# A two-layer decoder trunk: constants loaded between weights, a new pace of splits, scaling and rotation as queued steps

## The chip, the core and the metric

The kernel runs on one core of one Trainium2 chip. TensorE (PE) multiplies, VectorE (DVE), ScalarE (ACT) and GpSimd (POOL) do the rest, and SyncE (SP) issues every DMA, in order, on one queue. Every engine works through its own instructions in the order in which the program lists them; semaphores make one wait for another. The metric is the device time of one launch in microseconds.

## The reference, cut to what matters

```python
x <- LayerNorm(alpha * x + concat(A, B) @ w_out0)      # layer 0
x <- LayerNorm(alpha * x + concat(C, D) @ w_out1)      # layer 1
# A: gated linear attention over chunks, with a low-rank decay gate; B: spatial gating in chunks of 128
# C: retention over chunks of 128, q and k turned by rotary positions; D: causal pooling, windows 2, 4, 8, 16
# each branch times silu of a gate; all of them from one product h = x @ w_in of their layer
def _layer_norm(x, g, b):
    mu = mean(x); var = mean((x - mu) ** 2)
    return (x - mu) * rsqrt(var + 1e-5) * g + b
def _rotary(x, positions):
    return concatenate([x1 * cos - x2 * sin, x1 * sin + x2 * cos])
```

x is 2048 tokens of 1024 float32. The input product of layer 0 has 3088 columns, that of layer 1 has 3072, each output product 1024.

## The kernel before, in words

The 2048 tokens are worked through in four blocks of 512 (`NB`), each block through both layers before the next. A block has four token tiles of 128.

**Products.** All large products go through `unit` (L162). One call is a product with 512 columns (272 or 256 for layer 0's v), summed over eight k-tiles, for four output tiles. Each float32 operand is held as two parts in fp32r, a high one and the rest, and three products of parts (`PASSES`) make one. `width` says how many output tiles are built side by side, each in a PSUM bank of the pool "big" (four banks). After the matmuls of a group, `evac` is called for each of its output tiles, and then `between`.

**Weights.** All tiles of weights come in one list, `stream`, in the order of use: for each block eight tiles of 272 columns of wv, four pairs of 256 columns, then fourteen weights of eight tiles. `fetch` (L102) issues the load of the next one into a buffer of a pool of seven, shared with the loads of x. `cut` (L112) splits a landed tile: ScalarE writes the high part (L89), VectorE the rest (L90); then it fetches the next. There is room for twelve split tiles (`SLOTS`); `room` counts what is free. `pace` (L122), called after each k-tile of a product, adds a credit for the matmuls done and cuts one tile for each whole credit, as long as there is room. So splits stand in the queues of ScalarE and VectorE between the other work, at places that the program fixes.

**Steps.** `later(fn, delay)` puts a piece of work on a list. `between` (L145) counts every entry down by one, collects those that are due, in the order in which they were queued, and runs them. It is called after each group of output tiles, and inside a product of `width` over 1 also after every KT/width k-tiles. A step that is queued while steps run is not counted down in that call.

**The start.** Eight tiles of x and eight of wv are loaded in turn and split (L278). Then come the loads of pv and w_a2 (three copies), five fetches (the four pairs, of two DMAs each, and the first tile of the next weight), and seven more constants (L288 to L299). In block 0 the first product (wv, 272 columns) has width 4, so it fills all four banks; its `evac_v0` (L451) copies 16 columns of each bank three times on VectorE and 256 columns on ScalarE (L457). The second product (256 columns) follows.

**LayerNorm.** `layer_norm_out` (L207) runs the output product as two units of 512 columns. The first has width 2, the second width 1. `evac` of the second half of a token tile adds the residual (L217), takes the statistics (L218, L221), has GpSimd make 1/sqrt (L196, L199), and scales the row in two VectorE operations (L226 with mean and gain, L228 with 1/sqrt and bias). `after` follows: in layer 0 it queues `turn` (L620), which transposes the row on TensorE into two PSUM banks of a pool of two and splits them (L626 on ScalarE, L627 on VectorE), so that they are the input of layer 1; in layer 1 it stores the row.

**Rotation.** The first product of layer 1 (q and k, width 1) is evacuated by `evac_qk` (L639): a copy on ScalarE (L644), and six operations on VectorE (L645 to L654); then a transposing `turn` (L656) is queued with delay 3. The turns of token tiles 2 and 3 of the LayerNorm fall between the units of this product.

Of the kernel before, what the change touches and what calls it, by code (L numbers as in the profile page):

```python
# [13 lines left out]
ALU = mybir.AluOpType  # L14
# [3 lines left out]
P = 128  # L18
SEQ = 2048
D = 1024  # L20
KT = D // P
TB = 512
# [7 lines left out]
SLOTS = 12  # L30
# [21 lines left out]
def trunk(ctx, tc, x, xT, pos, wv, w, w_a2, pvec, rowp, sgu_rows, w_sT, w_pool, ropec, poolc, out):  # L52
    nc = tc.nc
# [20 lines left out]
    def big():  # L74
        return ps_big.tile([P, 512], F32, tag="big", name="big")
# [4 lines left out]
    def w2(name):  # L80
        return work.tile([P, TB], F32, tag="w2", name=name)
# [13 lines left out]
    for b in range(NB):  # L95
        stream += [(wv[kt, :, 0:272],) for kt in range(KT)]
        stream += [(wv[kt, :, 272:528], wv[kt + 1, :, 272:528]) for kt in range(0, KT, 2)]
        stream += [(w[g, kt],) for g in ORDER for kt in range(KT)]
    landed, ready = [], []
    room, credit = [SLOTS], [0.0]  # L100

    def fetch():  # L102
        if not stream:
            return
        src = stream.pop(0)
        raw = rawp.tile([P, 512], F32, tag="raw", name="raw")
        width = src[0].shape[1]
        for i, s in enumerate(src):
            nc.sync.dma_start(raw[:, i * width:(i + 1) * width], s)
        landed.append((raw, len(src), width))  # L110

    def cut():  # L112
        raw, n, width = landed.pop(0)
        assert room[0] > 0
        room[0] -= 1
        t = wpool.tile([P, 2, 512], F32R, tag="w", name="wt")
        c = n * width
        split(raw[:, 0:c], t[:, 0, 0:c], t[:, 1, 0:c])
        ready.extend((t[:, :, i * width:(i + 1) * width], i == n - 1) for i in range(n))
        fetch()  # L120

    def pace(matmuls):  # L122
        credit[0] = min(credit[0] + matmuls / 6.0, 2.0)
        while credit[0] >= 1.0 and room[0] > 0 and landed:
            cut()
            credit[0] -= 1.0

# [14 lines left out]
    def later(fn, delay=1):  # L142
        steps.append([delay, fn])
# [18 lines left out]
    def unit(xs, evac, token_major, width=2, cols=512):  # L162


        wt = []
        for n in range(0, 4, width):
            ps = [big()[:, 0:cols] for _ in range(width)]
            for kt in range(KT):
                if len(wt) == kt:
                    while not ready:  # L170
                        cut()
                    wt.append(ready.pop(0))
                t, last = wt[kt]
                for i, p_ in enumerate(ps):
                    sl = slice((n + i) * P, (n + i + 1) * P)
                    xt = xs[kt // 4][:, kt % 4]
                    for q, (a, b) in enumerate(PASSES):
                        lhsT, rhs = (xt[:, a, sl], t[:, b, :]) if token_major else (t[:, a, sl], xt[:, b, :])
                        nc.tensor.matmul(p_, lhsT=lhsT, rhs=rhs, start=(kt == 0 and q == 0),  # L179
                                         stop=(kt == KT - 1 and q == 2))  # L180
                if n + width == 4 and last:
                    room[0] += 1
                pace(3 * width * cols / 512.0)
                if width > 1 and (kt + 1) % (KT // width) == 0 and kt < KT - 1:
                    between()
            for i, p_ in enumerate(ps):
                evac(n + i, p_)
            between()
# [18 lines left out]
    def layer_norm_out(xs, rows, lnrow, after, cuts=1):  # L207
        ln = r8.tile([P, 2, D], F32, tag="r8", name="ln")
        for i in range(2):
            nc.sync.dma_start(ln[:, i, :], rowp[lnrow + i:lnrow + i + 1, :].broadcast_to([P, D]))  # L210
        gt, bt = ln[:, 0, :], ln[:, 1, :]
        sts = [small.tile([P, 2, 6], F32, tag="lnst", name="lnst", bufs=5) for _ in range(NT)]

        def evac(half, t, ps):
            row = rows[t // 2][:, t % 2, :]
            rh = row[:, half * 512:half * 512 + 512]
            nc.vector.scalar_tensor_tensor(rh, rh, ALPHA, ps, op0=ALU.mult, op1=ALU.add)  # L217
            nc.vector.bn_stats(sts[t][:, half, :], rh)  # L218
            if half == 1:
                mv = small.tile([P, 2], F32, tag="lnmv", name="lnmv")  # L220
                nc.vector.bn_aggr(mv, sts[t])  # L221
                rs = small.tile([P, 1], F32, tag="lnrs", name="lnrs")
                rstd(rs, mv[:, 1:2], LN_EPS)
                for c in range(0, D, D // cuts):
                    cs = slice(c, c + D // cuts)
                    nc.vector.scalar_tensor_tensor(row[:, cs], row[:, cs], mv[:, 0:1], gt[:, cs],  # L226
                                                   op0=ALU.subtract, op1=ALU.mult)
                    nc.vector.scalar_tensor_tensor(row[:, cs], row[:, cs], rs, bt[:, cs], op0=ALU.mult, op1=ALU.add)  # L228
                    after(t, row, cs)

        unit(xs, lambda t, ps: evac(0, t, ps), True)
        unit(xs, lambda t, ps: evac(1, t, ps), True, width=1)
# [24 lines left out]
    pv = const.tile([P, 20], F32, name="pv")  # L257
    gla_g, sgu_g, ret_g, pool_s, b_a = (pv[:, 4 * i:4 * i + 4] for i in range(5))
    wa2 = const.tile([48, 256], F32R, name="wa2")
    wsT = const.tile([P, 4, P], F32, name="wsT")  # L260
    wp = const.tile([P, 2, TB], F32R, name="wp")
    rope = const.tile([P, 32 + 10], F32, name="rope")
    poolt = const.tile([P, 4, 16], F32, name="poolt")
# [6 lines left out]
    pi_t = const.tile([P, 16], I32, name="pi_t")  # L270
    pf = const.tile([P, 16], F32, name="pf")

    wa2raw = w2("wa2raw")[0:48, 0:256]
    wraw, sb, sbs = w2("wraw"), w2("sgub"), w2("sgubs")
# [3 lines left out]
    for kt in range(KT):  # L278
# [3 lines left out]
        raw, _, width = landed.pop(0)  # L282
        t = wpool.tile([P, 2, 512], F32R, tag="w", name="wt")
# [1 line left out]
        room[0] -= 1  # L285
        ready.append((t[:, :, 0:width], True))

    nc.sync.dma_start(pv, pvec)  # L288
    for i in range(3):
        nc.sync.dma_start(wa2raw[16 * i:16 * i + 16, :], w_a2)  # L290
    for _ in range(5):
        fetch()
    nc.sync.dma_start(wsT, w_sT)
    nc.sync.dma_start(wraw, w_pool.rearrange("p g c -> p (g c)"))
    nc.sync.dma_start(sb, sgu_rows[0:1, :].broadcast_to([P, TB]))
    nc.sync.dma_start(sbs, sgu_rows[1:2, :].broadcast_to([P, TB]))
    nc.sync.dma_start(rope, ropec)
    nc.sync.dma_start(poolt, poolc)
    nc.sync.dma_start(pi_t, pos)  # L299

    def constants():

# [141 lines left out]
    def layer0(b, xs):  # L444
# [30 lines left out]
                nc.vector.tensor_copy(f[:, s, 3:4], e2[:, 3, 1:2])  # L475

        unit(xs, evac_v0, True, width=4 if b == 0 else 2, cols=272)
        if b == 0:
            constants()
            later(constants2, 3)  # L480
            later(constants3, 4)
# [137 lines left out]
        def after(t, row, cs):  # L619
            def turn():  # L620
                for c in range(2):
                    pt = tr()
                    for k in range(4):
                        nc.tensor.transpose(pt[:, k, :], row[:, (4 * c + k) * P:(4 * c + k + 1) * P], ident)  # L624
                    hi = x1[c][:, :, 0, t * P:(t + 1) * P]
                    nc.scalar.activation(hi, pt, AF.Copy)  # L626
                    nc.vector.tensor_tensor(x1[c][:, :, 1, t * P:(t + 1) * P], pt, hi.bitcast(F32), op=ALU.subtract)  # L627
            later(turn, 3)

        layer_norm_out([ca, cb], rows, 0, after)  # L630
        return x1, rows
# [1 line left out]
    def layer1(b, xs, rows):  # L633
# [3 lines left out]
        kst = [ks[t // 2][:, t % 2, :] for t in range(NT)]  # L637

        def evac_qk(t, ps):  # L639
            g = b * NT + t  # L640
            a = w2("ra")
            s_ = w2("rs_")

            nc.scalar.activation(a[:, 0:256], ps[:, 0:256], AF.Copy)  # L644
            nc.vector.tensor_tensor(a[:, 256:512].rearrange("p (h c) -> p h c", c=64),  # L645
                                    ps[:, 256:512].rearrange("p (h c) -> p h c", c=64),
                                    gam[:, 4:8].unsqueeze(2).broadcast_to([P, 4, 64]), op=ALU.mult)
            a3 = a.rearrange("p (h c) -> p h c", c=32)
            s3 = s_.rearrange("p (h c) -> p h c", c=32)
            nc.vector.tensor_tensor(s3, a3, sin[:, g:g + 1, :].broadcast_to([P, 16, 32]), op=ALU.mult)  # L650
            nc.vector.tensor_tensor(a3, a3, cos[:, g:g + 1, :].broadcast_to([P, 16, 32]), op=ALU.mult)
            nc.vector.tensor_tensor(a3[:, 0::2, :], a3[:, 0::2, :], s3[:, 1::2, :], op=ALU.subtract)
            nc.vector.tensor_tensor(a3[:, 1::2, :], a3[:, 1::2, :], s3[:, 0::2, :], op=ALU.add)
            nc.vector.tensor_copy(kst[t], a[:, 256:512])  # L654

            def turn():  # L656
                pt = tr()
                for s in range(4):
                    nc.tensor.transpose(pt[:, s, :], a[:, s * P:(s + 1) * P], ident)  # L659
                nc.scalar.activation(qkT[:, t], pt, AF.Copy)  # L660

            later(turn, 3)

        unit(xs, evac_qk, True, width=1)

# [91 lines left out]
        def after(t, row, cs):  # L757
            nc.sync.dma_start(out[b * TB + t * P:b * TB + (t + 1) * P, cs], row[:, cs])
# [90 lines left out]
```

## Time and profile before

| what | value |
|---|---|
| median of 3 runs | 1519.88 us (1518.55 to 1520.22) |
| the profiled execution | 1519.84 us, its span 1518.1 us, mean granted clock 0.993 |
| VectorE, ScalarE, GpSimd busy | 932.2, 554.9, 132.1 us |
| DMA | 162.18 MB, mean 107 GB/s |

The page of the profile gives each engine's busy time; the view of waits says who waited for whom, in total, how often and at most; the timeline lists instructions as start, duration, engine, line, operation, and in brackets the idle time before them with what ended it; the view of windows gives each engine's busy time in a stretch, then the granted clock, the DMA engines' busy share and GB/s. PEld is TensorE's weight load, SPq is the issuing of a DMA by SP.

### The profile page before, as it was taken

The numbers are of one execution on the slowest core, as the hardware profiler recorded it, in microseconds if no ns is written. First come the engines' busy times: TensorE is split into PE (matmuls) and PEld (weight loads), VectorE is DVE, ScalarE is ACT, GpSimd is POOL, SyncE is SP. The second block draws the span as 40 slices with busy tenths as digits, with TensorE's granted clock in tenths as the row PEclk, the third lists the DMA queues.
The fourth block names the chain that finished last, engine by engine and source line by source line (L and its number), as shares of the span: only waits on it lengthen the run. The fifth ranks groups of instructions, "written<-read, shape, count | busy, mean of one in ns | idle before, by whom it ended". The sixth has DMA issues, their size and how long they took to land.

```text
span 1518.1 us, 20883 instructions
## 1 busy us (share of the span) xinstructions
PE 1486.5 (98%) x7728; PEld 1247.3 (82%) x7728; DVE 932.2 (61%) x1860; ACT 554.9 (37%) x956; POOL 132.1 (9%) x184
## 2 busy tenths in 40 slices
PE   6999999999999999999999999999999999999997
PEld 6888878888988887888898888788889888878886
DVE  4486475657656558565675646847576554684756
ACT  5534323334443332324254332333426334142430
POOL 1020010100101001010001100101010110100001
PEclk8999999999999999999999999999999999999999
DMA  7323422224522442322453233131435315222321
GB/s 235 96 72 116 135 78 91 67 84 155 181 83 86 136 133 63 96 72 81 144 181 97 84 126 125 56 111 57 135 112 171 112 56 170 81 91 76 93 82 55
DMA packets 87046, 162.18 MB, mean 107 GB/s; under 512 B 10096, under 2 KB 18336, under 8 KB 86944
## 3 DMA queue, kind: packets, MB, share of 16 engines
q1 hardware_dynamic: 86944, 160.85, 33.3%
q8 instruction: 60, 0.98, 0.3%
q14 instruction: 42, 0.34, 0.1%
HBM read 152.43 MB, written 8.39 MB: 106 GB/s over the span
## 4 chain that ended last, share of the span: by engine, by line
PE 92%; DVE 3%; DMA 1%; POOL 1%; issue 1%; ACT 1%; SPq 0%; POOLq 0%; DVEq 0%; ACTq 0%
PE big L179 82%; PE att L356 4%; PE trp L392 1%; DVE wt L90 1%; PE trp L572 1%; PE trp L624 1%; PE trp L711 1%; POOL lnrs L196 1%; DMA raw<-in_w 1%; DVE T L627 1%; ACT wt L89 0%; DVE lnst L218 0%; PE trp L659 0%; PE trp L747 0%; PE trp L599 0%
## 5 line engine op out<-in xcount | busy, mean ns | idle before, releaser
L179 PE MATMUL big<-wt,T 128*128 128x512 f32 (+2 forms) x3456 | 728.1, 370 | 14.1 <-ACT v L457 9.5
L179 PEld LDWEIGHTS big<-wt,T 128*128 128x128 f32 x3456 | 601.0, 190 | 121.5 <-ACT v L457 9.7
L179 PE MATMUL big<-T,wt 128*128 128x512 f32 x2688 | 625.8, 391 | 0.0
L179 PEld LDWEIGHTS big<-T,wt 128*128 128x128 f32 x2688 | 500.6, 188 | 106.3 <-issue 2.7
L90 DVE TENSOR_TENSOR wt<-raw,wt 128x512 fp32r<-128x512 f32 (+1 forms) x496 | 320.8, 673 | 236.7 <-ACT wt L89 234.8
L89 ACT ACTIVATE wt<-raw 128x512 fp32r<-128x512 f32 (+1 forms) x496 | 298.3, 616 | 366.3 <-PE big L179 252.2
L196 POOL TENSOR_SCALAR lnrs<-lnmv 128x1 f32<-128x1 f32 x32 | 39.9, 1248 | 618.9 <-DVE lnmv L221 618.9
L217 DVE SCALAR_TENSOR_TENSOR rows<-rows,big 128x512 f32<-128x512 f32 x64 | 43.6, 681 | 53.6 <-PE big L179 53.6
L199 POOL TENSOR_TENSOR rs<-rs,neghalf 128x4 f32<-128x4 f32 x48 | 58.4, 1216 | 3.9
L228 DVE SCALAR_TENSOR_TENSOR rows<-rows,lnrs,ln 128x1024 f32<-128x1024 f32 (+1 forms) x36 | 42.0, 1166 | 24.9 <-POOL lnrs L199 24.8
L626 ACT ACTIVATE T<-trp 128x512 fp32r<-128x512 f32 x32 | 17.8, 596 | 82.3 <-PE trp L624 82.1
L218 DVE BATCH_NORM_STATS2 lnst<-rows 128x6 f32<-128x512 f32 x64 | 44.5, 695 | 2.2
L371 DVE COPY_PREDICATED pm<-mask,att 128x256 f32<-128x256 int32 x64 | 24.6, 439 | 30.8 <-PE att L356 30.8
L226 DVE SCALAR_TENSOR_TENSOR rows<-rows,lnmv,ln 128x1024 f32<-128x1024 f32 (+1 forms) x36 | 42.0, 1166 | 1.1
L204 DVE SCALAR_TENSOR_TENSOR y<-trp,pv,sg 128x512 f32<-128x512 f32 x48 | 33.7, 744 | 12.4 <-PE trp L599 7.0
L719 ACT ACTIVATE pb<-big 128x512 f32<-128x512 f32 x16 | 9.4, 590 | 76.4 <-PE big L179 76.4
L584 ACT ACTIVATE act<-big 128x512 f32<-128x512 f32 x32 | 18.3, 597 | 51.7 <-PE big L179 50.9
L682 DVE BATCH_NORM_STATS2 st<-att 128x6 f32<-128x128 f32 x64 | 14.2, 285 | 35.4 <-PE att L356 35.4
L356 PEld LDWEIGHTS att<-v,pm 128*128 128x128 f32 x256 | 33.5, 191 | 2.4
L550 DVE BATCH_NORM_STATS2 st<-zt 128x6 f32<-128x128 f32 x64 | 13.7, 277 | 35.1 <-ACT zt L546 35.1
L89 ACT ACTIVATE T<-y 128x512 fp32r<-128x512 f32 x48 | 29.4, 627 | 15.7 <-DVE y L204 15.3
L724 DVE TENSOR_TENSOR pl<-pb 128x527 f32<-128x527 f32 x16 | 11.3, 708 | 38.6 <-ACT pb L719 37.8
(184 smaller groups left out, 905.8 us busy)
## 6 DMA issues: line engine op xcount, KB each, us to landing
raw<-in_w SPq DMA_DIRECT2D x448, 256.0 KB, 2.8
xraw<-in_xT SPq DMA_DIRECT2D x32, 256.0 KB, 3.5
rows<-in_x SPq DMA_DIRECT2D x8, 1024.0 KB, 7.1
ln<-in_rowp SPq DMA_DIRECT2D x16, 512.0 KB, 6.4
out<-rows SPq DMA_DIRECT2D x12, 512.0 KB, 2.7
raw<-in_wv SPq DMA_DIRECT2D x32, 136.0 KB, 3.2
raw<-in_wv SPq DMA_DIRECT2D x32, 128.0 KB, 2.8
out<-rows SPq DMA_DIRECT2D x8, 256.0 KB, 2.0
```

Source lines behind the costliest of these rows:

```text
L89: nc.scalar.activation(hi, src, AF.Copy)
L90: nc.vector.tensor_tensor(lo, src, hi.bitcast(F32), op=ALU.subtract)
L179: nc.tensor.matmul(p_, lhsT=lhsT, rhs=rhs, start=(kt == 0 and q == 0), stop=(kt == KT - 1 and q == 2))
L196: nc.gpsimd.tensor_scalar(dst, var, eps, None, op0=ALU.add)
L199: nc.gpsimd.tensor_tensor(dst, dst, neghalf[:, :n], op=ALU.pow)
L204: nc.vector.scalar_tensor_tensor(y, psT, gain, sil, op0=ALU.mult, op1=ALU.mult)
L217: nc.vector.scalar_tensor_tensor(rh, rh, ALPHA, ps, op0=ALU.mult, op1=ALU.add)
L218: nc.vector.bn_stats(sts[t][:, half, :], rh)
L226: nc.vector.scalar_tensor_tensor(row[:, cs], row[:, cs], mv[:, 0:1], gt[:, cs], op0=ALU.subtract, op1=ALU.mult)
L228: nc.vector.scalar_tensor_tensor(row[:, cs], row[:, cs], rs, bt[:, cs], op0=ALU.mult, op1=ALU.add)
L356: nc.tensor.matmul(dst, lhsT=lhsT, rhs=rhs, start=start, stop=stop, skip_group_check=True)
L371: nc.vector.copy_predicated(pm[t % 2][:, r::2, :], mask_b, ps[r][:, 2:4, :])
```

## The change

Four things are altered:
- Constants. A list `small_loads` is filled after the loads of x and wv, and each later `fetch` issues one of its loads behind its own. Its order is w_a2 (three), pv, wraw, wsT, sb, sbs, rope, poolt, pos.
- Pace. `cut` is held back while `room` is not over `hold`, which is set to SLOTS - KT - KT//2 at the start and to 0 after the first product of each block. In a product of width 4 the credit of a k-tile is 0.75 instead of 3·width·cols/512/6.
- LayerNorm. The two scaling operations and `after` become a step, `scale`, queued with delay 1. The first of them takes the whole row; the second is still cut in `cuts` pieces.
- Rotation. All of `evac_qk` becomes a step, `rotate`, queued with delay 1. Both kinds of `turn`, now queued from inside a step, get delay 2 instead of 3.

```diff
-    landed, ready = [], []
-    room, credit = [SLOTS], [0.0]
+    landed, ready, small_loads = [], [], []
+    room, credit, hold = [SLOTS], [0.0], [0]
...
         landed.append((raw, len(src), width))
+        if small_loads:
+            nc.sync.dma_start(*small_loads.pop(0))
...
-        while credit[0] >= 1.0 and room[0] > 0 and landed:
+        while credit[0] >= 1.0 and room[0] > hold[0] and landed:
...
-                pace(3 * width * cols / 512.0)
+                pace(3 * width * cols / 512.0 if width < 4 else 0.75 * 6)
...
-                for c in range(0, D, D // cuts):
-                    cs = slice(c, c + D // cuts)
-                    nc.vector.scalar_tensor_tensor(row[:, cs], row[:, cs], mv[:, 0:1], gt[:, cs],
-                                                   op0=ALU.subtract, op1=ALU.mult)
-                    nc.vector.scalar_tensor_tensor(row[:, cs], row[:, cs], rs, bt[:, cs], op0=ALU.mult, op1=ALU.add)
-                    after(t, row, cs)
+
+                def scale():
+                    nc.vector.scalar_tensor_tensor(row, row, mv[:, 0:1], gt, op0=ALU.subtract, op1=ALU.mult)
+                    for c in range(0, D, D // cuts):
+                        cs = slice(c, c + D // cuts)
+                        nc.vector.scalar_tensor_tensor(row[:, cs], row[:, cs], rs, bt[:, cs],
+                                                       op0=ALU.mult, op1=ALU.add)
+                        after(t, row, cs)
+
+                later(scale)
...
-    nc.sync.dma_start(pv, pvec)
-    for i in range(3):
-        nc.sync.dma_start(wa2raw[16 * i:16 * i + 16, :], w_a2)
+    small_loads += [(wa2raw[16 * i:16 * i + 16, :], w_a2) for i in range(3)]
+    small_loads += [(pv, pvec), (wraw, w_pool.rearrange("p g c -> p (g c)")), (wsT, w_sT),
+                    (sb, sgu_rows[0:1, :].broadcast_to([P, TB])), (sbs, sgu_rows[1:2, :].broadcast_to([P, TB])),
+                    (rope, ropec), (poolt, poolc), (pi_t, pos)]
     for _ in range(5):
         fetch()
-    nc.sync.dma_start(wsT, w_sT)
-    nc.sync.dma_start(wraw, w_pool.rearrange("p g c -> p (g c)"))
-    nc.sync.dma_start(sb, sgu_rows[0:1, :].broadcast_to([P, TB]))
-    nc.sync.dma_start(sbs, sgu_rows[1:2, :].broadcast_to([P, TB]))
-    nc.sync.dma_start(rope, ropec)
-    nc.sync.dma_start(poolt, poolc)
-    nc.sync.dma_start(pi_t, pos)
+    hold[0] = SLOTS - KT - KT // 2
...
         unit(xs, evac_v0, True, width=4 if b == 0 else 2, cols=272)
+        hold[0] = 0
...
-            later(turn, 3)
+            later(turn, 2)
...
         def evac_qk(t, ps):
+            later(lambda: rotate(t, ps))
+
+        def rotate(t, ps):
...
-            later(turn, 3)
+            later(turn, 2)
```

## The prediction

> **What bounds the kernel now.** I read the engines' busy shares first, then TensorE's own waits.
>
> ```profile
> PE 1486.5 (98%) x7728; PEld 1247.3 (82%) x7728; DVE 932.2 (61%) x1860; ACT 554.9 (37%) x956; POOL 132.1 (9%) x184
> ```
> ```profile
> PE big L179 <- ACT v L457: 9.5, 1, 9.5
> PE trp L624 <- DVE T L627: 8.7, 4, 2.2
> PE big L179 <- ACT wt L89: 4.5, 1, 4.5
> ```
>
> TensorE (PE) is busy for 98% of the span; of the 31.6 us in which it is not, 22.7 are these three waits. The change adds and removes no matmul, so it can only touch these waits, the clock lost through them, and the tail after the last matmul. The first and the third wait lie in the first 30 us, the second is one stall of 2.2 us in each of the four blocks. So next comes the timeline of those places.
>
> ```profile
> 10.75 0.42 SPq L288 DMA_DIRECT2D pv<-in_pvec  x1
> 11.23 1.35 SPq L290 DMA_DIRECT2D wa2raw<-in_w_a  x3
> 5.22 14.30 PE L179 MATMUL big<-wt,T 128*128 128x272 f32 x95 [0.17 <-DVE wt L90]
> 12.68 3.69 SPq L109 DMA_DIRECT2D raw<-in_wv  x8
> 16.47 0.38 SPq L109 DMA_DIRECT2D raw<-in_w  x1
> 17.36 0.43 SPq L294 DMA_DIRECT2D wraw<-in_w_pool  x1
> 19.44 0.63 ACT L89 ACTIVATE wt<-raw 128x512 fp32r<-128x512 f32 x1 [1.05 <-DMA raw<-in_wv]
> 20.90 0.63 ACT L89 ACTIVATE wt<-raw 128x512 fp32r<-128x512 f32 x1 [0.84 <-DVE wt L90]
> 21.18 37.90 SPq L109 DMA_DIRECT2D raw<-in_w  x19
> 25.55 1.88 ACT L89 ACTIVATE wt<-raw 128x512 fp32r<-128x512 f32 x3 [4.02 <-DMA raw<-in_w]
> 28.55 1.48 ACT L457 ACTIVATE v<-big 128x256 f32<-128x256 f32 x4 [1.11 <-DVE alr L455]
> 28.98 5.28 PE L179 MATMUL big<-wt,T 128*128 128x256 f32 x24 [9.46 <-ACT v L457]
> 34.46 3.11 PE L179 MATMUL big<-wt,T 128*128 128x256 f32 x24
> ```
>
> The first product's matmuls end at 19.5. Its four PSUM banks are the pool's only four, so the second product waits for ScalarE's copy of the first bank, 28.55. ScalarE runs in order, and ahead of that copy stand the splits that the pace released during the first product. Credit was 3·4·272/512/6 = 1.06 per k-tile, so eight: four pairs of wv and four tiles of the next weight. The last three start at 25.55, after 4.02 us of waiting for tiles whose load was issued at 21.18, behind seven constants on SP's queue.
>
> **Part 1, constants and pace.** First what the diff's words don't do. The gate is `hold = SLOTS-KT-KT//2` = 12-8-4 = 0, so `room > hold` is the old condition. Only the credit changes the number: 0.75 per k-tile gives cuts at k-tiles 1, 2, 3, 5, 6 and 7, six instead of eight: the four pairs and the first two tiles of the next weight. The copy now waits for the second of those, not the fourth.
>
> When does that tile land? SP's issues up to the first tile keep their number and only change order: 10.75 + 3.69 (eight halves) + 1.77 (pv and wa2) is 16.2, against 16.47 before. After it come wraw and then the second tile, so that tile takes about the place that wraw had before, issued at 17.36:
>
> ```profile
> wraw<-in_w_pool SPq DMA_DIRECT2D x1, 256.0 KB, 4.7
> ```
>
> 17.36 + 4.7 = 22.1, less the 0.2 of earlier issue: 21.9. The ends are the start of the first tile's split, 20.9 (below it would have to overtake that one), and 25.5, where it was split before. I take 21.9, as the same bytes stand ahead of it as stood ahead of wraw. From a last split's start to PE's restart the rows give 28.98 - (25.55+1.88-0.63) = 2.2: the split on ScalarE, the low part on VectorE, the small copies there, the copy of the bank. So PE restarts at 21.9 + 2.2 = 24.1 instead of 28.98: **-4.9 us** (ends -5.9 and -1.3).
>
> Then the clock. These windows end with the granted clock, DMA share and GB/s:
>
> ```profile
> 22.00:24.00 2.00, 0.00 (x0) 0.00 (x0) 0.34 (x1) 0.00 (x0) 0.98 (x3) 0.91 0.92 267
> 32.00:34.00 2.00, 2.00 (x12) 2.00 (x12) 0.00 (x0) 0.00 (x0) 0.00 (x0) 0.53 0.85 253
> 220.00:240.00 20.00, 17.82 (x82) 14.70 (x81) 14.53 (x26) 3.65 (x9) 1.88 (x2) 0.91 0.24 76
> ```
>
> The 0.91 and 0.53 of the first two put the drop to half at 23.6 and the return at 33.9. The first 24 matmuls after the stall took 5.28, the next 24 took 3.11: 2.2 us lost. With a restart at 24.1 the idle stretch is still 4.6 us and the clock has just dropped. The last window, in block 0's first LayerNorm, held (1-0.91)·20/0.5 = 3.6 us at half clock after a stall of 2.2; a stretch like it from 23.6 ends at 27.2 and costs (27.2-24.1)/2 = 1.5. **-0.7 us** (0 if it stays low as long as before, -2.2 if it doesn't drop). The Trainium skill ("TensorE: Matmul & The Clock Gate", sections "What's actually happening" and "HAM oscillation") ties the drop to idle gaps over about 3.4 us, in a window that runs free of the kernel; by it too the remaining gap drops the clock, but the 2.2 us stalls below would not, and there the trace differs (0.91 in block 0).
>
> The six constants still left (wsT, sb, sbs, rope, poolt, pi_t) now go one behind each later fetch. Each holds SP for about 0.43, and the 256 KB ones hold the next tile back. I cost that at nothing. The eight tiles of this weight are first multiplied after the second product, 96 matmuls of which 24 take 3.11, so not before 24.1 + 4·3.11 = 36.5. Nine transfers of 256 KB follow the second tile up to the eighth, an estimated 1.0 us each at the 267 GB/s above, so they end before 31. Without that cover each constant would cost its 0.43 of issue or more.
>
> **Part 2, LayerNorm's scaling and the rotation.** PE and VectorE (DVE) around block 0's first LayerNorm, then block 1's PE:
>
> ```profile
> 210.58 5.73 PE L179 MATMUL big<-wt,T 128*128 128x512 f32 x24
> 216.94 5.70 PE L179 MATMUL big<-wt,T 128*128 128x512 f32 x24
> 224.82 1.82 PE L624 MATMUL trp<-ident,rows 128*128 128x128 f32 x8 [2.18 <-DVE T L627]
> 226.29 6.72 PE L179 MATMUL big<-wt,T 128*128 128x512 f32 x24
> 233.65 5.74 PE L179 MATMUL big<-wt,T 128*128 128x512 f32 x24
> 590.24 5.70 PE L179 MATMUL big<-wt,T 128*128 128x512 f32 x24
> 599.14 5.71 PE L179 MATMUL big<-wt,T 128*128 128x512 f32 x24
> ```
> ```profile
> 216.14 3.09 DVE L90 TENSOR_TENSOR wt<-raw,wt 128x512 fp32r<-128x512 f32 x5
> 219.15 0.68 DVE L217 SCALAR_TENSOR_TENSOR rows<-rows,big 128x512 f32<-128x512 f32 x1
> 220.83 1.28 DVE L226 SCALAR_TENSOR_TENSOR rows<-rows,lnmv,ln 128x1024 f32<-128x1024 f32 x1
> 222.88 1.28 DVE L228 SCALAR_TENSOR_TENSOR rows<-rows,lnrs,ln 128x1024 f32<-128x1024 f32 x1 [0.77 <-POOL lnrs L199]
> 224.08 1.28 DVE L627 TENSOR_TENSOR T<-trp,T 128x512 fp32r<-128x512 f32 x2
> 225.28 1.88 DVE L90 TENSOR_TENSOR wt<-raw,wt 128x512 fp32r<-128x512 f32 x3
> 227.09 0.42 DVE L645 TENSOR_TENSOR ra<-big,rope 128x256 f32<-128x256 f32 x1
> 229.99 1.28 DVE L627 TENSOR_TENSOR T<-trp,T 128x512 fp32r<-128x512 f32 x2
> ```
>
> The turn of tile 2 needs the two transpose banks, which the turn of tile 1 gives back with its subtractions at 224.08. PE wanted them at 224.82 - 2.18 = 222.64. In front of the subtractions stands tile 3's scaling, from 220.83 to 224.08, with 0.77 of it spent waiting for GpSimd (POOL).
>
> `later(scale)` has delay 1 and falls due in the `between` right after the same evacuation. Steps run in the order they were queued, and the turn is older, so turn, then scale. The turn's delay of 2, counted from inside that `between`, is the old 3: PE's order is unchanged. On DVE, tile 2's GpSimd wait is now filled by a turn (-0.77), so tile 3's evacuation starts at 218.4, its statistics take the old 1.68, and the subtractions run 220.1 to 221.3: 1.3 us before PE needs the banks. The stall goes.
>
> Its worth: a product of 24 with a turn takes 216.94 - 210.58 = 6.36. In block 0 the two after it took 9.35 and 7.36, so 2.99 + 1.00 lost, the 1.00 at half clock. In block 1 it was 8.90, so 2.54; blocks 2 and 3 share the row of four stalls with longest 2.2, so I count three of 2.54. **-11.6 us**, 10.2 of it without clock if another execution shows no drop here.
>
> What is late next: the scaling of tile 3 moves to 221.3-223.8, its turn is due at about 229; the three splits end at 225.7 and tile 2's subtractions at 227.0, needed by its product at 222.64 + 0.8 + 5.7 + 0.8 = 229.9; the rotation of tile 0, 2.9 us of DVE as between 227.09 and 229.99, ends about 229.9, where before, and its transposes come after another product. So 2.9 us of slack on the nearest. Moving the rotation behind the turn alone buys nothing on PE and is costed at 0; its cover is that slack. The bank of the product is held longer, by a turn, but its next user is four products away.
>
> **The tail.**
>
> ```profile
> 1511.16 0.75 DVE L226 SCALAR_TENSOR_TENSOR rows<-rows,lnmv,ln 128x512 f32<-128x512 f32 x1
> 1511.21 0.78 POOL L196 TENSOR_SCALAR lnrs<-lnmv 128x1 f32<-128x1 f32 x1 [4.00 <-DVE lnmv L221]
> 1514.12 0.75 DVE L228 SCALAR_TENSOR_TENSOR rows<-rows,lnrs,ln 128x512 f32<-128x512 f32 x1
> 211.74 1.31 POOL L196 TENSOR_SCALAR lnrs<-lnmv 128x1 f32<-128x1 f32 x1 [3.48 <-DVE lnmv L221]
> ```
>
> In the last block the first scaling operation now covers the whole row, 1.28 for two of 0.75. One half-row operation leaves the chain after the GpSimd wait: -0.75. But the GpSimd operation beside it takes 0.78 next to a half row and 1.31 next to a whole one, so the wait ends 0.53 later. **-0.2 us**. The Trainium skill ("SBUF — State Buffer", section "Who interferes with whom") has a VectorE instruction with two SBUF inputs block a GpSimd instruction that reads SBUF for its whole length. The two durations agree; without that rule the tail would give -0.75.
>
> **Sum.** 4.9 + 0.7 + 11.6 + 0.2 = 17.4. The profiled execution took 1519.84 (span 1518.1), the median of the runs is 1519.88, so they can be used alike: 1519.84 - 17.4 = **1502.4**.
>
> **Rivals.**
> - *The start gains nothing* (0.14): the words "no early splits" don't hold, six remain, and the second tile lands as late as tiles did before, because the loads saturate (0.92 of the DMA engines above). Against it: it now stands ahead of six constants. 1519.84 - 11.8 = 1508.0.
> - *The start gains more* (0.08): tiles land so early that the fourth pair's split, 19.44, is the last that matters. Restart at 21.6, no lasting drop: 7.4 + 2.2, 1498.4.
> - *The turn's stall stays* (0.08): the subtractions are over 1.3 us later than I count, for instance through splits that wait for late tiles. With all four: 1519.84 - 5.8 = 1514.0.
> - *Slower* (0.03): the rotations, now behind turns, back DVE up until tile 2's and 3's low parts hold up the products. It decides from 2.9 us of lateness; each further us costs four. To eat 17.4 it takes 2.9 + 4.4 = 7.3 us, two and a half rotations. At 8 us late: 1502.4 + 4·5.1 = 1522.8. Nothing adds work to DVE, which speaks against it.
>
> The forecast itself has 0.67. Range 1498.4 to 1508.0: it takes in both cases of the start and leaves out the last two and some of the clock's chance. A measurement here tells about 0.2%, 3 us, from no change: faster 0.96, same 0.02, slower 0.02.
>
> **What would show it.** PE's waits after: no row of a turn waiting for DVE; DVE's order in tile 3 statistics, two subtractions, then scaling; one wait for ScalarE's copy of 4 to 5 us instead of 9.5, ended at 23.5 to 24.5; a clock of 1.00 around 220; the last GpSimd operation of 1.3. It is wrong if the copy is still behind three splits, if a turn still waits, or if PE gains a new row, for a weight tile or for a low part.

## The result and the profile after

The changed kernel takes 1503.9 us (median of 4 runs, 1503.26 to 1505.25) against 1519.39 for the kernel before in runs beside it (1518.55 to 1520.22): a ratio of 0.9899, 95% interval 0.9882 to 0.9916. The profiled execution took 1503.44, its span 1501.7, so 16.4 less than the one before. The forecast was 1502.4, in a range of 1498.4 to 1508.0.

TensorE's waits after the change, in the same columns as before (total, times, longest):

```profile
PE big L181 <- ACT v L458: 5.9, 1, 5.9
PE big L181 <- ACT wt L89: 4.6, 1, 4.6
PE big L181 <- DVE wt L90: 0.2, 1, 0.2
```

The row of the turns is gone. The wait for ScalarE's copy is 5.9 instead of 9.5, the first wait for data is about what it was (4.6, before 4.5). No new row has come in.

The timeline of the start after the change, SP's issues, ScalarE's last early split and copy, and the restart:

```profile
11.30 0.80 SPq L109 DMA_DIRECT2D raw<-in_wv  x2
...
16.91 1.10 SPq L109 DMA_DIRECT2D raw<-in_w  x1
18.06 0.43 SPq L112 DMA_DIRECT2D wraw<-in_w_pool  x1
18.59 0.38 SPq L109 DMA_DIRECT2D raw<-in_w  x1
...
22.73 0.63 ACT L89 ACTIVATE wt<-raw 128x512 fp32r<-128x512 f32 x1 [1.77 <-DMA raw<-in_w]
24.48 1.59 ACT L458 ACTIVATE v<-big 128x256 f32<-128x256 f32 x4 [1.11 <-DVE alr L456]
24.91 4.97 PE L181 MATMUL big<-wt,T 128*128 128x256 f32 x24 [5.94 <-ACT v L458]
```

One split (22.73) instead of three stands last before the copy, and from its start to PE's restart it is 24.91 - 22.73 = 2.2 us, as forecast. But the tile came later than forecast, at 22.7 instead of 21.9. PE restarts 4.1 us earlier than before (24.91 for 28.98), while its wait shrank by 3.5 (5.94 for 9.46), because the first product also ended 0.55 earlier in this execution.

VectorE and then TensorE at block 0's first LayerNorm, and two rows of block 1:

```profile
213.94 0.68 DVE L219 SCALAR_TENSOR_TENSOR rows<-rows,big 128x512 f32<-128x512 f32 x1
214.66 0.69 DVE L220 BATCH_NORM_STATS2 lnst<-rows 128x6 f32<-128x512 f32 x1
215.38 0.21 DVE L223 BATCH_NORM_AGGREGATE lnmv<-lnst 128x2 f32<-128x12 f32 x1
215.51 1.24 DVE L629 TENSOR_TENSOR T<-trp,T 128x512 fp32r<-128x512 f32 x2
216.66 1.27 DVE L228 SCALAR_TENSOR_TENSOR rows<-rows,lnmv,ln 128x1024 f32<-128x1024 f32 x1
218.04 1.28 DVE L231 SCALAR_TENSOR_TENSOR rows<-rows,lnrs,ln 128x1024 f32<-128x1024 f32 x1
219.24 1.89 DVE L90 TENSOR_TENSOR wt<-raw,wt 128x512 fp32r<-128x512 f32 x3
221.05 1.28 DVE L629 TENSOR_TENSOR T<-trp,T 128x512 fp32r<-128x512 f32 x2
222.25 0.41 DVE L650 TENSOR_TENSOR ra<-big,rope 128x256 f32<-128x256 f32 x1
```
```profile
212.57 5.71 PE L181 MATMUL big<-wt,T 128*128 128x512 f32 x24
218.12 1.04 PE L626 MATMUL trp<-ident,rows 128*128 128x128 f32 x8
218.91 5.73 PE L181 MATMUL big<-wt,T 128*128 128x512 f32 x24
224.48 1.04 PE L626 MATMUL trp<-ident,rows 128*128 128x128 f32 x8
225.27 5.71 PE L181 MATMUL big<-wt,T 128*128 128x512 f32 x24
```
```profile
582.12 5.71 PE L181 MATMUL big<-wt,T 128*128 128x512 f32 x24
...
588.46 5.73 PE L181 MATMUL big<-wt,T 128*128 128x512 f32 x24
```

VectorE's order is tile 3's statistics, the two subtractions of tile 1's turn, then scaling, then splits, tile 2's subtractions, rotation. The subtractions end at 216.75, 1.4 us before PE's transposes at 218.12, those of tile 2's turn. A product with its turn takes 6.34 to 6.36 now where it had taken 9.35 and 8.90.

### The profile page after: what moved, and what is told of

Read it like the earlier page. It is cut to its first block, busy times and chain, and to the rows that moved or that the text cites. A ratio compares the mean times of both kernels' runs of the same rounds, so it can differ in the third digit from the quotient of the medians.

```text
span 1501.7 us, 20886 instructions
## 1 busy us (share of the span) xinstructions
PE 1482.5 (99%) x7728; PEld 1246.0 (83%) x7728; DVE 930.1 (62%) x1856; ACT 551.5 (37%) x956; POOL 125.1 (8%) x184
## 4 chain that ended last, share of the span: by engine, by line
PE 96%; DMA 2%; DVE 1%; issue 0%; POOL 0%; ACT 0%; SPq 0%; DVEq 0%; POOLq 0%; ACTq 0%
PE big L181 86%; PE att L357 4%; PE trp L393 1%; PE trp L574 1%; PE trp L626 1%; PE trp L716 1%; DMA xraw<-in_xT 1%; DMA raw<-in_w 1%; PE trp L664 0%; PE trp L752 0%; PE trp L601 0%; DVE wt L90 0%; DMA raw<-in_wv 0%; PE trp L507 0%; SPq L109 0%
## 5 line engine op out<-in xcount | busy, mean ns | idle before, releaser
L198 POOL TENSOR_SCALAR lnrs<-lnmv 128x1 f32<-128x1 f32 x32 | 33.4, 1042 | 618.3 <-DVE lnmv L223 618.3
L228 DVE SCALAR_TENSOR_TENSOR rows<-rows,lnmv,ln 128x1024 f32<-128x1024 f32 x32 | 41.0, 1283 | 0.9
## 6 DMA issues: line engine op xcount, KB each, us to landing
ln<-in_rowp SPq DMA_DIRECT2D x16, 512.0 KB, 6.3
out<-rows SPq DMA_DIRECT2D x12, 512.0 KB, 2.7
```

The source lines that it names most:

```text
L198: nc.gpsimd.tensor_scalar(dst, var, eps, None, op0=ALU.add)
L228: nc.vector.scalar_tensor_tensor(row, row, mv[:, 0:1], gt, op0=ALU.subtract, op1=ALU.mult)
```

## The experiments

To place a gain I compare the start of the same matmul in two traces: their order on TensorE is the same in all kernels here. For the changed kernel against the one before, the second product starts 4.1 us earlier, the third 4.4, and over the four LayerNorms of layer 0 the lead grows by 4.0, 2.6, 2.6 and 2.6; the last matmul ends 16.2 earlier, the span 16.4.

A single trace leaves the start uncertain by about a microsecond. With the old start, PE restarts at 28.98 (the kernel before), 29.31 (rotation alone) and 29.93 (scaling alone); with the new one at 24.91 (the changed kernel), 25.23 (start alone) and 25.46 (a late VectorE).

My theory was that the scaling behind the turn gives all of the LayerNorm part and the rotation nothing, and that at the start the number of early splits and the order of the loads work only together. The rivals were that the rotation carries a part, and that either half of the start's change is enough by itself.

**Scaling alone.** The kernel before with `scale` as a step and the delay of 2 in the turn of a LayerNorm's row:

```diff
-                for c in range(0, D, D // cuts):
...
+                later(scale)
...
-            later(turn, 3)
+            later(turn, 2)
```

> Scaling as a step (with the turn's delay 2) on the kernel before, nothing else. Theory S (the LayerNorm part's whole gain is the scaling moved behind the turn): TensorE's wait for VectorE at the turns goes from 8.7 us in four stalls to 0, about 11.3 us less, 1508. The rotation then stands in front of tile 2's subtractions, whose slack I reckon at 0, so up to 0.5 us per block may come back. Rival R (the rotation as a step carries part of it): 3 us or more of the 11.3 is missing, 1511 or above, with a new wait of a product for a low part.

1510.39 (1508.90 to 1511.51), ratio 0.9938, interval 0.9921 to 0.9954: between the two expectations. The row of the turns' waits is gone. TensorE and VectorE at the same place in this kernel:

```profile
223.80 1.04 PE L628 MATMUL trp<-ident,rows 128*128 128x128 f32 x8
224.59 5.73 PE L179 MATMUL big<-wt,T 128*128 128x512 f32 x24
230.38 1.25 PE L628 MATMUL trp<-ident,rows 128*128 128x128 f32 x8
231.39 5.73 PE L179 MATMUL big<-wt,T 128*128 128x512 f32 x24
```
```profile
226.73 0.42 DVE L649 TENSOR_TENSOR ra<-big,rope 128x256 f32<-128x256 f32 x1
...
229.64 1.28 DVE L631 TENSOR_TENSOR T<-trp,T 128x512 fp32r<-128x512 f32 x2
```

Tile 2's turn (223.80) follows its product at once. But tile 3's turn now meets the rotation: the rotation of tile 0 stands in front of tile 2's subtractions, which run at 229.64 instead of right after the splits, so the second bank comes back late and the transposes take 1.25. From product to product it is 231.39 - 224.59 = 6.80, 0.44 over 6.36, in each block. So the scaling is worth about 9.9 of the 11.7 us, and the rotation's move 4·0.44 = 1.8, once the first stall is gone. That is the "up to 0.5" of theory S, and a part of rival R.

**Rotation alone.** The kernel before with `later(lambda: rotate(t, ps))` and the delay of 2 in its own turn:

> The rotation alone as a step on the kernel before. Theory S: the four stalls of 2.2 us at the turns stay, time within 1.5 us of the kernel before. Rival R: the stalls shrink, 2 us or more off.

1517.64 in one run. The stalls stay:

```profile
PE trp L624 <- DVE T L627: 8.7, 4, 2.2
```

The time is 2.0 under the median of the kernel before beside it (1519.65, 1518.19 to 1522.29), more than the 1.5 that I allowed theory S and by its size as rival R had it, but R's sign, smaller stalls, is absent. Of the 2.2 us that its span is shorter, 1.5 lie at block 0's turn, whose stretch ran at the full clock in this execution, and 0.5 at the start, where the product restarts 0.3 later but its first 24 matmuls take 4.44 instead of 5.28. So there is no sign that the rotation by itself gives anything; one run can't exclude a few tenths.

**The start alone.** Constants, `hold` and the pace, with LayerNorm and rotation as before:

> Constants between weights and the pace of 0.75, LayerNorm and rotation as before. Theory: the second product starts at 24 to 25 as in the changed kernel, 4.0 to 5.0 us less, about 1515; the stalls at the turns stay at 8.7 us in total. Rival (the parts depend on one another): the gain is under 3 us.

1515.82 (10 runs, 1513.33 to 1517.67), ratio 0.9973, interval 0.9964 to 0.9982. The second product starts at 25.23, 3.75 us earlier and just behind the 24 to 25 expected, and the stalls at the turns are still 8.7.

**The order of the loads alone.** The same with the old pace, `pace(3 * width * cols / 512.0)`, so eight early splits:

> Constants between weights, but the old pace of eight splits in the first product. Theory N (number and order act together: the copy waits for the last early split, whose tile is the fourth of the next weight): in the changed kernel that tile landed at 26.8, so the second product starts at 29 as before, gain under 1 us. Rival O (the order of the loads alone gives the start's gain): the second product starts at about 25, 4 us less.

1518.91 in one run. ScalarE and TensorE in it:

```profile
26.64 0.63 ACT L89 ACTIVATE wt<-raw 128x512 fp32r<-128x512 f32 x1 [1.27 <-DMA raw<-in_w]
28.38 1.48 ACT L454 ACTIVATE v<-big 128x256 f32<-128x256 f32 x4 [1.11 <-DVE alr L452]
28.82 3.57 PE L181 MATMUL big<-wt,T 128*128 128x256 f32 x15 [9.76 <-ACT v L454]
```

The last early split, of the fourth tile, starts at 26.64, and the product at 28.82, 0.16 before the earliest of the three restarts with the old start. Rival O falls.

**The number of splits alone.** The kernel before with `pace(... if width < 4 else 0.75 * 6)`:

> The pace of 0.75 (six splits) with the constants in their old place. Theory N (number and order act together): the last early split waits for the second tile, still loaded behind seven constants and landing at 25.5, so the second product starts at about 27.7, 1.3 us less than before. Rival P (the number alone gives the start's gain): a start at about 25, 4 us less.

1518.99 in one run.

```profile
26.18 0.63 ACT L89 ACTIVATE wt<-raw 128x512 fp32r<-128x512 f32 x1 [4.45 <-DMA raw<-in_w]
...
28.35 4.00 PE L179 MATMUL big<-wt,T 128*128 128x256 f32 x17 [8.95 <-ACT v L457]
```

Six splits, but the tile of the sixth is still behind seven constants: ScalarE waits 4.45 for it, and the product starts at 28.35, 0.6 us before that same earliest restart, where theory N had 27.7. Rival P falls too. Each half gives 0.2 to 0.6 by itself, in one trace each and inside the spread of a microsecond; both together give 3.8 to 4.1, well beyond it. The copy waits for the last early split, and with six splits that one comes early only if it is an earlier tile and the tile is loaded early. With four, the order may matter less, since the fourth pair's split starts at 19.44 in the kernel before and at 19.40 in the changed one; no run has four splits with the old order.

**Four early splits.** If so, the two splits that are left in front of the copy are still a cost. The changed kernel with

```diff
-                pace(3 * width * cols / 512.0 if width < 4 else 0.75 * 6)
+                pace(3 * width * cols / 512.0 if width < 4 else 0.5 * 6)
```

> The changed kernel with credit 0.5 instead of 0.75, so four early splits, the pairs alone. Theory: the copy of the banks waits only for the fourth pair, split at 19.4 in the changed kernel, so the second product starts at 19.4 + 2.2 = 21.6 instead of 24.9: 3.3 us less plus up to 2 of clock, about 1499.5. Rival (another wait takes its place: the next weight's tiles are split too late, or the copy waits for something else): less than 1.5 us, with a new TensorE wait for a weight tile.

1498.87 (1497.27 to 1500.62), ratio to the kernel before 0.9863, interval 0.9843 to 0.9884.

```profile
18.40 0.63 ACT L89 ACTIVATE wt<-raw 128x512 fp32r<-128x512 f32 x1 [0.61 <-DMA raw<-in_wv]
20.15 1.48 ACT L458 ACTIVATE v<-big 128x256 f32<-128x256 f32 x4 [1.11 <-DVE alr L456]
20.58 3.14 PE L181 MATMUL big<-wt,T 128*128 128x256 f32 x24 [0.75 <-ACT v L458]
```

The last split starts at 18.40, a microsecond earlier than I had it, and the restart is again 2.2 later. PE is idle for 0.75, and its first 24 matmuls take 3.14 instead of the 4.97 and 5.28 of the two kernels: the clock did not drop. Its four runs fall in two pairs: 1497.27 and 1497.40 with a mean granted clock of 0.999, 1500.34 and 1500.62 with 0.997. A clock lower by 0.002 over 1499 us makes about 3 us, the distance between the pairs; no trace of the slower pair shows where it was lost.

**Three early splits.** The same line with `0.375 * 6`:

> Credit 0.375, three early splits; the fourth pair is split after the copies. Theory: the copies start when the first product ends, at 18.9 to 19.4, the second product at about 20, an idle gap under 1.5 us that drops no clock: 5 us of start and about 2 of clock against the changed kernel, about 1497. Rival: the second product now waits for its fourth pair or the third product for its last tiles, and the time is 1500 or above.

1497.31 (1497.12 to 1497.72), ratio to the kernel before 0.9853, interval 0.9832 to 0.9874: the lowest median here, and 6.05 us under the changed kernel in the profiled executions (1497.39 against 1503.44). The wait for the copy is no longer listed. The rival is seen in a small form: the row of waits for a split now counts two, the 4.4 of the start and one of 0.54.

```profile
PE big L181 <- ACT wt L89: 5.0, 2, 4.4
```
```profile
40.30 1.14 ACT L89 ACTIVATE wt<-raw 128x512 fp32r<-128x512 f32 x2
...
40.97 5.35 PE L181 MATMUL big<-T,wt 128*128 128x512 f32 x21 [0.54 <-ACT wt L89]
```

The third product waits 0.54 us for a tile whose split stands behind the gate's exponentials on ScalarE. With that, three splits and four come out alike in the profiled spans (1495.7 both).

**A late VectorE.** The changed kernel, with n+1 additions of no use in block n, to find the slack. They stand behind tile 3's statistics, so in front of the subtractions of tile 1's turn; TensorE meets them at tile 2's turn. (`normed[0]` counts the LayerNorms of layer 0; the lines that do so are left out.)

```diff
+                if lnrow == 0 and t == NT - 1:
+                    late = w2("late")
+                    for _ in range(normed[0]):
+                        nc.vector.tensor_tensor(late, gt[:, 0:512], bt[:, 0:512], op=ALU.add)
                 later(scale)
```

> The changed kernel with 1, 2, 3 and 4 useless VectorE additions of 0.69 us (each about 0.61 to 0.72 apart) put in front of tile 3's turn in blocks 0, 1, 2 and 3. Theory S: in the changed kernel the subtractions end 1.4 us before TensorE wants the banks, so one addition costs nothing, two cost 0 to 0.1, three about 0.6, four about 1.3 us of a TensorE wait for VectorE at the turn; in all about 2 us. Rival (TensorE was not held by these subtractions): no wait in any block.

1505.33 in one run. TensorE in block 2 (three additions) and block 3 (four), then block 3's subtractions:

```profile
951.86 5.70 PE L181 MATMUL big<-wt,T 128*128 128x512 f32 x24
957.54 1.26 PE L633 MATMUL trp<-ident,rows 128*128 128x128 f32 x8
958.55 3.68 PE L181 MATMUL big<-wt,T 128*128 128x512 f32 x15
```
```profile
1321.47 5.70 PE L181 MATMUL big<-wt,T 128*128 128x512 f32 x24
1327.89 1.25 PE L633 MATMUL trp<-ident,rows 128*128 128x128 f32 x8 [0.71 <-DVE T L636]
1328.90 5.71 PE L181 MATMUL big<-wt,T 128*128 128x512 f32 x24
```
```profile
1327.15 1.28 DVE L636 TENSOR_TENSOR T<-trp,T 128x512 fp32r<-128x512 f32 x2
```

From product to product it is 6.34 with two additions, 6.69 with three and 7.43 with four: 0, 0.35 and 1.09 us lost. So VectorE does hold TensorE here, from a delay of 1.4 to 2.1 us on. The losses are a quarter of a microsecond under my figures, since the first bank comes back after the first of the two subtractions: in block 3 the transposes start at 1327.89, in the middle of the two (1327.15 to 1328.43).

## Why the prediction was right, and where its sizes were off

**The turn's stall** was forecast at -11.6. By the matmuls' starts it gave 4.0 + 3·2.6 = 11.7: right in cause and size, and the extra in block 0 is the clock, as stated. That extra, 1.5 of the 11.7, belongs to the execution of the kernel before: of the five traces with these stalls four lost it once and one, the rotation alone, never. The subtractions were forecast to end 1.3 us before PE's need; it was 1.4.

**"Moving the rotation behind the turn alone buys nothing on PE and is costed at 0"** holds for the kernel before, as the run of the rotation alone shows. Inside the change it is the step that was mis-sized: 1.8 of the 11.7 are the rotation's. I had worked the slack out with the rotation already moved and not asked what it was without. Nor was 2.9 us the nearest slack: tile 3's transposes want the banks of tile 2's turn back 0.8 us before the product that I counted to, so by the prediction's own figures it was 229.1 - 227.0 = 2.1. In the changed kernel tile 2's subtractions end at 222.33 and those transposes start at 224.48.

**The start's restart** was forecast at -4.9 and gave -4.1. The mechanism was right: six splits, not "no early splits", and the copy behind the second tile. But the copy's wait was 5.9 and ended at 24.91, outside the 4 to 5 and the 23.5 to 24.5 that the prediction named as signs. The mis-sized term is the second tile's load. I had its issue at 17.2 and its split's start at 21.9; they were at 18.59 and 22.73. SP issued the first pair at 11.30 instead of 10.75, since it waits for a buffer of the split before, and the first tile's issue took 1.10. But a late issue is not all of it. In the run of the start alone the issue began near my figure, and the split came later still:

```profile
17.68 1.41 SPq L109 DMA_DIRECT2D raw<-in_w  x1
...
22.96 0.63 ACT L89 ACTIVATE wt<-raw 128x512 fp32r<-128x512 f32 x1 [1.98 <-DMA raw<-in_w]
```

What these traces, and that of the late VectorE, share is one issue of over a microsecond at the second tile or just in front of it. In the kernel before such an issue fell behind the place that I took for this tile (17.36), so my estimate left it out:

```profile
18.32 1.34 SPq L296 DMA_DIRECT2D sgubs<-in_sgu_rows  x1
```

Whether such an issue alone makes the tile late, and why an issue takes so long, is open.

**The clock at the start** was forecast at -0.7 and gave -0.3: the first 24 matmuls after the stall took 4.97 instead of 5.28. The mis-sized term is the length of the stretch at half clock: I had it from 23.6 to 27.2. By these two windows it lasted from 22.3 to 29.1:

```profile
22.00:24.00 2.00, 0.00 (x0) 0.00 (x0) 0.60 (x1) 0.63 (x1) 0.00 (x0) 0.57 0.99 286
28.00:30.00 2.00, 2.00 (x15) 1.99 (x14) 0.27 (x1) 0.00 (x0) 0.00 (x0) 0.72 0.92 315
```

So 4.2 us of work ran at half clock behind the restart, where the kernel before had 4.9. This gain is also smaller than what executions of one start differ by: with the old start the same 24 matmuls took 4.44 (rotation alone), 5.28 (the kernel before) and 5.49 (scaling alone).

**The tail** was forecast at -0.2, and the span is 0.2 shorter than the last matmul's end explains. After, its GpSimd operation is

```profile
1495.06 1.31 POOL L198 TENSOR_SCALAR lnrs<-lnmv 128x1 f32<-128x1 f32 x1 [3.48 <-DVE lnmv L223]
```

1.31 as forecast, where it was 0.78 before. Together the parts make 4.1 + 0.3 + 11.7 + 0.2 = 16.3 of the span's 16.4 us.

**The rivals.** The start gained 4.1, not nothing; the stall did not stay and nothing became slower. "The start gains more" named the version that the runs with three and four splits then made: 7.4 of restart and 2.2 of clock were priced, for 1498.4.

## What to carry to other kernels

Work that is issued ahead of its need on an in-order engine makes everything behind it wait for the newest of its data: count which transfer the last such piece waits for, and where that transfer is one whose place you can change, both the number of pieces and the order of the transfers must fit. When a stall is due to the order on a helper engine, put what hands back a buffer first and what nobody waits for last, and work out the slack of each reordering as it stands without the others. A gate written as an expression is worth evaluating: `hold` was 0 here, so it held nothing back, and three splits fewer were worth another 6 us.

## What the runs showed of the hardware

The same GpSimd operation took three durations, by what VectorE did beside it. Beside the scaling of a whole row it takes 1.31 (1495.06 above), beside that of half a row 0.78 (1511.21 in the kernel before), beside the turn's subtractions, one of whose inputs is in PSUM, it takes

```profile
207.37 0.22 POOL L198 TENSOR_SCALAR lnrs<-lnmv 128x1 f32<-128x1 f32 x1 [3.48 <-DVE lnmv L223]
```

So the reordering also took VectorE's wait for GpSimd away at tiles 2 and 3. The Trainium skill ("SBUF — State Buffer", section "Who interferes with whom") says that two SBUF inputs on VectorE block a GpSimd read and a single one doesn't; both cases agree.

The stall of 2.2 us at block 0's turn dropped the clock in the kernel before (granted 0.91 between 220 and 240) and not in the run of the rotation alone, whose window shows the same idle time at the full clock:

```profile
220.00:240.00 20.00, 17.81 (x89) 14.50 (x88) 15.01 (x28) 4.90 (x11) 1.88 (x2) 1.00 0.22 69
```

Five traces have four such stalls each: the kernel before, the rotation alone, the start alone and each half of the start. Four of the 20 stalls halved the clock, each for 3.41 us: in block 0 of the kernel before, of the start alone and of the number of splits alone, and in block 1 of the order of the loads alone. The traces also keep the times at which the granted clock changes, and within a trace they lie whole multiples of 3.41 us apart (at the start it was low for 6.83 in the changed kernel and for 10.24 in the kernel before). Laid on that grid, the four stalls that halved the clock put 2.1 to 2.2 us of idle time into one interval; the other 16 were cut in two by a grid point, with at most 1.9 us in one interval. So where a stall falls on the grid decides whether it costs clock, and the grid lies differently in each execution. That agrees with the Trainium skill's window that runs free of the kernel ("TensorE: Matmul & The Clock Gate", section "What's actually happening"); that it takes a whole idle window of about 3.4 us, as the same section has it, does not hold here.
